# Attention output of a two-block model on one core: split value and probability parts in fp32r, transposes one key block ahead, convolution taps moved

## The chip, the cores and the metric

The kernel runs on one core of one Trainium2 chip. The metric is the time of one execution on the device in microseconds (us). TensorE (PE) does the matrix products and the transposes, VectorE (DVE) and ScalarE (ACT) the elementwise work, SyncE (SP) issues the weight loads.

## The reference, cut to what matters

The model has a first block (gated delta rule heads and pooling, not touched here) and a second block of two layers. Each layer of the second block is a feed-forward part, a mixer, a second feed-forward part and a gated projection, on 512 tokens of width 1024 in float32. The mixer is this:

```python
def forgetting_attention(q, k, v, f_logit):          # 8 heads of 64, 512 tokens
    c = jnp.cumsum(jax.nn.log_sigmoid(f_logit), axis=1)
    for blk in range(s // Q_BLOCK):                  # 4 query blocks of 128
        sc = q_blk @ k[:qe].T * scale + (c_q - c_k)  # causal: keys up to qe
        pr = jax.nn.softmax(where(causal, sc, -inf), axis=-1)
        outs.append(pr @ v[:qe])
...
y_attn = forgetting_attention(q, k, v, f_logit) @ w_attn_out
y_conv = silu(rmsnorm(depthwise_conv31(a * sigmoid(b)))) @ w_conv_out   # 512 channels, 31 taps
merged = sigmoid(z_ga) * y_attn + sigmoid(z_gc) * y_conv
return merged @ w_out
```

## The kernel before

Activations lie transposed, 128 channels on the partitions and 512 tokens along the free axis. A weight product is three fp32r products (`mm3`, lines 156 to 158): each float32 operand is split into a high part, rounded to fp32r, and a low part, the rest, and high by high, low by high and high by low are added in PSUM. The weights stream through `Stream`: SP loads a group, ACT casts the high part (`whi`, line 108), DVE subtracts for the low part (`wlo`, line 109).

In `mixer` the order of the code is: four `glu` steps that make the inputs of the convolution, the value product over all heads (`vps`, lines 500 to 507), the copy of the four value tiles from PSUM (`vt`, line 510, one ACT instruction of 512 columns for each), the forget gate (`pf`, lines 513 to 528), then four pairs of heads (`heads`, hp 0 to 3). After these come 16 gate products and 16 output products (`gate`, `part`), interleaved with a distance of `AHEAD` = 3, then `w_out`.

The convolution is 124 DVE instructions a layer ("taps", lines 414 and 419; four channel blocks of 31). They are put into the code in portions: `TAPS0` = 12 after each `glu`, `TAPSV` = 8 after the value product, `TAPS1` = 1, 1, 2, 1 behind the four score blocks of each pair of heads, `TAPS2` = 12 behind each of the attention's output products, and what is left in `conv_out` (line 562), which then squares, sums, normalises, applies silu and splits the result into `yh` and `yl`. `conv_out` stands ahead of part number `CONV_AT` = 5. The first product that reads `yh` and `yl` is part 8.

A pair of heads has two stages. The score stage runs over four query blocks: for each head a score product in two fp32r instructions (`sc`, lines 452 and 454) and a mask product (458), a maximum (DVE, 460), an exponential with its sum (ACT, 462), a reciprocal (463) and a scaling (467). The output stage runs over four key blocks: float32 transposes of the probabilities into PSUM (`pt`, line 477, ten for each head), a DVE copy into SBUF (481), and a float32 product for each head into 64 rows of one PSUM tile (`o`, line 485), so that the two heads take two column halves of the array. Each of these float32 products stands in the trace as two load and matmul pairs. At the end `split` writes the high and low parts `oh` and `ol` (168, 169).

`FILL` says how many steps of the next pair's query and key products (`qk_steps`, 16 steps; for the last pair 8 steps of the first gate product) the code puts behind each score block and each key block. PSUM has two pools of four banks each: `acc` (`psum`) for the weight products, `aux` (`paux`) for scores, transposes and, before, the attention output. The temporaries (`tmp`, among them the gates) share six slots.

The framework in which the kernel is written decides the final order of each engine's instructions when it is built: it follows the order of the code, and pulls later work forward where its plan has an engine free. So the code gives precedence, not the final order. On the chip each engine then works through its list in that order.

Of the kernel before, what the change touches and what calls it, by code (L numbers as in the profile page):

```python
# [7 lines left out]
F32 = mybir.dt.float32  # L8
F32R = mybir.dt.float32r
AF = mybir.ActivationFunctionType  # L10
ALU = mybir.AluOpType
PSUM = bass.MemoryType.PSUM

P = 128
# [6 lines left out]
GRP = 8  # L21
UNIT = 4
AHEAD = 3
ENG2 = dict(pe="v", dup="a", pt="vv")
BANKS2 = (4, 4)
TAPS0 = 12
TAPSV = 8
GATES0 = 1
FILL = (3, 4, 3, 0, 1, 2, 1, 2)
TAPS1 = (1, 1, 2, 1)  # L30
TAPS2 = 12
CONV_AT = 5
NEG = -float(2 ** 100)
EPS = 1e-6

# [117 lines left out]
def mm3(nc, ps, w, x, start, stop):  # L153
    wh, wl = w
    xh, xl = x
    nc.tensor.matmul(ps, lhsT=wh, rhs=xh, start=start, stop=False)  # L156
    nc.tensor.matmul(ps, lhsT=wh, rhs=xl, start=False, stop=False)  # L157
    nc.tensor.matmul(ps, lhsT=wl, rhs=xh, start=False, stop=stop)  # L158
# [8 lines left out]
def split(nc, hi, lo, src):  # L167
    nc.scalar.copy(hi, src)
    nc.vector.tensor_tensor(lo, src, hi.bitcast(F32), op=ALU.subtract)
# [7 lines left out]
def block2(tc, kk, W, h, xp, x0, sq0, p_t, par, out_t):  # L177


    nc = tc.nc  # L180
    with ExitStack() as ctx:
# [15 lines left out]
        def tmp(name="t", shape=(P, S), dt=F32):  # L197
            return tp.tile(list(shape), dt, tag="t", name=name, bufs=NB)

        def psum(name):  # L200
            return acc.tile([P, S], F32, tag="acc", name=name)

        def paux(name, shape=(P, S)):
            return aux.tile(list(shape), F32, tag="aux", name=name)
# [21 lines left out]
        def mtile(i, name, dt=F32R):  # L226
            return mp.tile([P, S], dt, tag=f"m{i}", name=name)
# [37 lines left out]
        def proj(name, l, col, ps=None, k_n=KD, x=None):  # L265
            ps = psum("pj") if ps is None else ps
            x = (xh, xl) if x is None else x
            for k in range(k_n):
                w = W.get((name, l, k * P, col))
                mm3(nc, ps, w, (x[0][k], x[1][k]), k == 0, k == k_n - 1)  # L270
            return ps
# [86 lines left out]
        def gt(i, hl, name):  # L358
            return gp.tile([P, S], F32R, tag=f"g{hl}{i}", name=name)

        def mixer(l, after):
            R = norm()
            oh = [gt(i, "h", f"oh{i}") for i in range(4)]
            ol = [gt(i, "l", f"ol{i}") for i in range(4)]
# [27 lines left out]
            def dup(dst, src):  # L392
                if ENG2["dup"] == "a":
                    nc.scalar.copy(dst, src)
                elif ENG2["dup"] == "p":
                    nc.gpsimd.tensor_copy(dst, src)
                else:
                    nc.vector.tensor_copy(dst, src)
# [29 lines left out]
            def taps(n):  # L428

                while n > 0 and done[0] < 31 * len(ca):  # L430
                    next(conv)
                    done[0] += 1
                    n -= 1
                if done[0] == 124:
                    next(conv, None)

            def heads(hp, qk1, filler):

                rr = [slice(64 * i, 64 * i + 64) for i in range(2)]

                def fill(n):
                    for _ in range(n):
                        next(filler, None)

                pp = [[], []]
                for qb in range(4):
                    n = (qb + 1) * P
                    qs = slice(qb * P, qb * P + P)
                    pss = [paux("sc") for i in range(2)]
                    for i, ps in enumerate(pss):  # L450
                        q, k = qk1[i]
                        nc.tensor.matmul(ps[:, :n], lhsT=q[:, qs], rhs=k[:, :n], start=True, stop=False)
                        q, k = qk2[hp % 2][i]
                        nc.tensor.matmul(ps[:, :n], lhsT=q[:, qs], rhs=k[:, :n], start=False, stop=False)
                    fill(FILL[qb])
                    for i, ps in enumerate(pss):
                        o = ps[:, :n]
                        nc.tensor.matmul(ps[:, qs], lhsT=kk.identr, rhs=maskr, start=False, stop=True)
                        sm = sp.tile([P, 4], F32, tag="sm", name="sm", bufs=4)
                        nc.vector.tensor_reduce(sm[:, 0:1], o, axis=mybir.AxisListType.X, op=ALU.max, negate=True)  # L460
                        pe = cp.tile([P, n], F32, tag=f"pe{qb}", name="pe", bufs=2)
                        nc.scalar.activation(pe, o, AF.Exp, bias=sm[:, 0:1], accum_out=sm[:, 1:2])
                        nc.vector.reciprocal(sm[:, 2:3], sm[:, 1:2])
                        if ENG2["pe"] == "a":
                            nc.scalar.activation(pe, pe, AF.Copy, scale=sm[:, 2:3])
                        else:
                            nc.vector.tensor_scalar(pe, pe, sm[:, 2:3], None, op0=ALU.mult)
                        pp[i].append(pe)
                    taps(TAPS1[qb])
                po_ = paux("o")  # L470
                for kb in range(4):
                    n = S - kb * P
                    pts = []
                    for i in range(2):
                        ps = paux("pt")
                        for qb in range(kb, 4):
                            nc.tensor.transpose(ps[:, (qb - kb) * P:(qb - kb) * P + P], pp[i][qb][:, kb * P:kb * P + P],
                                                kk.ident)
                        t = mtile(8 + kb % 2 * 4 + 2 * i, "pt", F32)[:, :n]
                        copy = nc.scalar.copy if ENG2["pt"][i] == "a" else nc.vector.tensor_copy  # L480
                        copy(t, ps[:, :n])
                        pts.append(t)
                    fill(FILL[4 + kb])
                    for i, r in enumerate(rr):
                        nc.tensor.matmul(po_[r, kb * P:], lhsT=vt[kb][:, hp * P + 64 * i:hp * P + 64 * i + 64], rhs=pts[i],  # L485
                                         start=kb == 0, stop=kb == 3)
                split(nc, oh[hp], ol[hp], po_)

            for cb in range(4):
                glu(cb)  # L490
# [3 lines left out]
            for t in range(4):  # L494
                nc.tensor.matmul(pst[:, 2 * t:2 * t + 2], lhsT=st.sq[:, t * P:t * P + P],
                                 rhs=kk.ones[1024][:, 0:2], start=True, stop=True)
            Rt = sp.tile([P, 8], F32, tag="Rt", name="Rt")
            rstd(Rt, pst)

            vps = [psum(f"v{t}") for t in range(4)]  # L500
            for k in range(KD):
                wh, wl = W.get(("w_in_2", l, k * P, 1024), 4)
                for t in range(4):
# [1 line left out]
                    nc.tensor.matmul(vps[t], lhsT=xh[k][:, ts], rhs=wh, start=k == 0, stop=False)  # L505
                    nc.tensor.matmul(vps[t], lhsT=xl[k][:, ts], rhs=wh, start=False, stop=False)
                    nc.tensor.matmul(vps[t], lhsT=xh[k][:, ts], rhs=wl, start=False, stop=k == KD - 1)
            vt = [mtile(t, f"vt{t}", F32) for t in range(4)]
            for t in range(4):
                nc.scalar.activation(vt[t], vps[t], AF.Copy, scale=Rt[:, 2 * t:2 * t + 1])  # L510
            taps(TAPSV)

            pf = proj("f_2", l, 0)
            z = tmp("z")[0:72]
            nc.vector.tensor_tensor(z, pf[0:72], R[0:72], op=ALU.mult)
            bf = par[0:72, po["b_f"][0] + l:po["b_f"][0] + l + 1]
# [1 line left out]
            e = tmp("e")[0:72]  # L518
# [5 lines left out]
            c = tmp("c")[0:72]  # L524
# [15 lines left out]
            def gate(i):  # L540
                for _ in gate_steps(i):
                    pass
# [8 lines left out]
            for hp in range(4):  # L551
                nxt = [], []
# [9 lines left out]
            def conv_out():  # L562
                taps(200)
                sq = tmp("ysq")
                nc.scalar.activation(sq, y[0], AF.Square)
                for cb in range(1, 4):
                    t = tmp("ysqm")
                    nc.scalar.activation(t, y[cb], AF.Square)
                    nc.vector.tensor_tensor(sq, sq, t, op=ALU.add)
                Rc = norm(sq, 512)  # L570
                yh = [mtile(8 + t, f"yh{t}") for t in range(4)]
                yl = [mtile(12 + t, f"yl{t}") for t in range(4)]
                for cb in range(4):
                    nc.vector.scalar_tensor_tensor(y[cb], y[cb], pcol("g_conv", l, cb), Rc, op0=ALU.mult, op1=ALU.mult)
                    nc.scalar.activation(y[cb], y[cb], AF.Silu)
                    split(nc, yh[cb], yl[cb], y[cb])
                ysp[:] = yh, yl
# [19 lines left out]
            for i in range(2 * KD + AHEAD):  # L597
                if GATES0 <= i < 2 * KD:
                    gate(i)
                if i == CONV_AT + AHEAD:  # L600
                    conv_out()
                if i >= AHEAD:
                    part(i - AHEAD)
            for m in range(KD):
                ps = proj("w_out_2", l, m * P, x=(mh, ml))
# [37 lines left out]
        v = sp.tile([P, 4], F32, name="lv")  # L643
        r = sp.tile([P, 4], F32, name="lr")
# [3 lines left out]
        for m in range(KD):  # L648
            t = tmp("fin")
# [929 lines left out]
```

## Time and profile before

| | |
|---|---|
| median of 3 runs | 2983.38 us (2982.89 to 2984.37) |
| the profiled execution's own time | 2982.64 us |
| its span, first to last instruction | 2980.9 us |
| mean granted TensorE clock | 0.995 |
| PE, DVE, ACT busy, share of the span | 98%, 64%, 44% |

The heads of layer 1 lie at about 1178 to 1269 us of the span, those of layer 2 at about 2297 to 2388 us. A matmul's busy time overlaps that of the next one; what it costs TensorE is the distance from its start to the start of the next instruction. Starts in a row are in us from the span's start; the "idle before" in brackets is the time that the engine had been idle, and what ended it.

### The profile page before, as it was taken

The numbers are of one execution on the slowest core, as the hardware profiler recorded it, in microseconds if no ns is written. First come the engines' busy times: TensorE is split into PE (matmuls) and PEld (weight loads), VectorE is DVE, ScalarE is ACT, GpSimd is POOL, SyncE is SP. The second block draws the span as 40 slices with busy tenths as digits, with TensorE's granted clock in tenths as the row PEclk, the third lists the DMA queues.
The fourth block names the chain that finished last, engine by engine and source line by source line (L and its number), as shares of the span: only waits on it lengthen the run. The fifth ranks groups of instructions, "written<-read, shape, count | busy, mean of one in ns | idle before, by whom it ended". The sixth has DMA issues, their size and how long they took to land.

```text
span 2980.9 us, 37957 instructions
## 1 busy us (share of the span) xinstructions
PE 2935.6 (98%) x13980; PEld 2393.3 (80%) x13980; DVE 1914.2 (64%) x3778; ACT 1302.4 (44%) x2395; POOL 48.1 (2%) x105
## 2 busy tenths in 40 slices
PE   7999999999999999999999999999999999999998
PEld 4888888778888887688888888888888688888886
DVE  6788888777544469886543447544469886543446
ACT  5667766435323335544432335323335544432333
POOL 1000000000000000000000000000000000000000
PEclk9999999999999999999999999999999999999999
DMA  5211123332333332123333333333332123233232
GB/s 202 67 46 46 45 57 106 93 92 90 94 99 95 97 99 85 50 85 99 93 99 99 95 96 101 98 99 97 95 99 84 50 87 99 92 99 99 93 99 85
DMA packets 112970, 268.77 MB, mean 90 GB/s; under 512 B 43536, under 2 KB 47120, under 8 KB 112784
## 3 DMA queue, kind: packets, MB, share of 16 engines
q1 hardware_dynamic: 111760, 266.28, 28.9%
q8 instruction: 110, 1.80, 0.3%
q14 instruction: 76, 0.62, 0.1%
q0 software_dynamic: 1024, 0.07, 0.0%
HBM read 262.17 MB, written 4.06 MB: 89 GB/s over the span
## 4 chain that ended last, share of the span: by engine, by line
PE 95%; DVE 2%; ACT 2%; issue 1%; DMA 0%; DVEq 0%; SPq 0%; ACTq 0%
PE pj L158 17%; PE pj L156 17%; PE pj L157 17%; PE fo L156 5%; PE fo L158 5%; PE fo L157 5%; PE px L156 3%; PE px L157 3%; PE px L158 3%; PE o L485 1%; PE wo L157 1%; PE mP L1268 1%; PE mX L1263 1%; PE wo L158 1%; PE wo L156 1%; PE chn L1315 1%
## 5 line engine op out<-in xcount | busy, mean ns | idle before, releaser
L108 ACT CAST whi<-wraw 128x512 fp32r<-128x512 f32 x914 | 567.0, 621 | 1158.5 <-PE pj L157 700.3
L109 DVE TENSOR_TENSOR wlo<-wraw,whi 128x512 fp32r<-128x512 f32 x914 | 627.4, 687 | 449.4 <-ACT whi L108 427.0
L157 PE MATMUL pj<-xl,whi 128*128 128x512 f32 x1712 | 673.3, 393 | 0.0
L156 PE MATMUL pj<-xh,whi 128*128 128x512 f32 x1712 | 671.1, 392 | 0.9 <-DVE h L1504 0.9
L158 PE MATMUL pj<-xh,wlo 128*128 128x512 f32 x1712 | 670.2, 391 | 0.0
L158 PEld LDWEIGHTS pj<-xh,wlo 128*128 128x128 f32 x1712 | 322.2, 188 | 67.8 <-issue 2.3
L157 PEld LDWEIGHTS pj<-xl,whi 128*128 128x128 f32 x1712 | 322.3, 188 | 66.8 <-issue 2.7
L156 PEld LDWEIGHTS pj<-xh,whi 128*128 128x128 f32 x1712 | 322.4, 188 | 65.9 <-ACT whi L108 1.3
L157 PE MATMUL fo<-gl,whi 128*128 128x512 f32 x704 | 274.1, 389 | 0.0
L158 PE MATMUL fo<-gh,wlo 128*128 128x512 f32 x704 | 274.1, 389 | 0.0
L156 PE MATMUL fo<-gh,whi 128*128 128x512 f32 x704 | 274.1, 389 | 0.0
L419 DVE SCALAR_TENSOR_TENSOR cy<-ca,par,cy 128x489 f32<-128x489 f32 (+17 forms) x240 | 169.5, 729 | 1.5
L157 PE MATMUL px<-xl,whi 128*128 128x512 f32 x392 | 160.3, 409 | 0.0
L158 PE MATMUL px<-xh,wlo 128*128 128x512 f32 x392 | 160.0, 408 | 0.0
L156 PE MATMUL px<-xh,whi 128*128 128x512 f32 x392 | 159.2, 406 | 0.0
L158 PEld LDWEIGHTS fo<-gh,wlo 128*128 128x128 f32 x704 | 132.2, 188 | 27.4
L157 PEld LDWEIGHTS fo<-gl,whi 128*128 128x128 f32 x704 | 132.2, 188 | 27.4
L156 PEld LDWEIGHTS fo<-gh,whi 128*128 128x128 f32 x704 | 132.2, 188 | 27.3
L340 DVE TENSOR_TENSOR fb<-pj,R 128x512 f32<-128x512 f32 x88 | 60.8, 691 | 129.3 <-PE pj L158 129.3
L337 DVE TENSOR_TENSOR fa<-pj,R 128x512 f32<-128x512 f32 x88 | 60.8, 691 | 125.2 <-PE pj L158 123.2
L156 PE MATMUL pj<-nh,whi 128*128 128x512 f32 x352 | 137.5, 391 | 0.0
L157 PE MATMUL pj<-nl,whi 128*128 128x512 f32 x352 | 137.2, 390 | 0.0
(431 smaller groups left out, 4486.3 us busy)
## 6 DMA issues: line engine op xcount, KB each, us to landing
wraw<-in_w_dram SPq DMA_DIRECT2D x465, 512.0 KB
mw<-in_w_dram SPq DMA_DIRECT2D x16, 512.0 KB
raw<-in_xt_dram SPq DMA_DIRECT2D x8, 256.0 KB
h<-in_xt_dram SPq DMA_DIRECT2D x8, 256.0 KB
out_dram<-fin SPq DMA_DIRECT2D x8, 256.0 KB
rawc<-in_ctxt_dram SPq DMA_DIRECT2D x2, 512.0 KB
db<-B SPq DMA_DIRECT2D x64, 6.0 KB
Pm<-dq SPq DMA_DIRECT2D x64, 12.0 KB
```

The costliest lines, as they stand in the source:

```text
L108: nc.scalar.copy(hi, src)
L109: nc.vector.tensor_tensor(lo, src, hi.bitcast(F32), op=ALU.subtract)
L156: nc.tensor.matmul(ps, lhsT=wh, rhs=xh, start=start, stop=False)
L157: nc.tensor.matmul(ps, lhsT=wh, rhs=xl, start=False, stop=False)
L158: nc.tensor.matmul(ps, lhsT=wl, rhs=xh, start=False, stop=stop)
L337: nc.vector.tensor_tensor(a, pa, R, op=ALU.mult)
L340: nc.vector.tensor_tensor(b, pb, R, op=ALU.mult)
L419: nc.vector.scalar_tensor_tensor(yy[:, s:], ca[cb][:, :S - s], pcol("conv_w", l, cb, j), yy[:, s:], op0=ALU.mult, op1=ALU.add)
L485: nc.tensor.matmul(po_[r, kb * P:], lhsT=vt[kb][:, hp * P + 64 * i:hp * P + 64 * i + 64], rhs=pts[i], start=kb == 0, stop=kb == 3)
L1263: nc.tensor.matmul(pX[:, o], lhsT=st.B[:, m0 + m], rhs=alt(st.Q, m0 + m), start=True, stop=True)
L1268: nc.tensor.matmul(pP[:, o], lhsT=Xt[:, m], rhs=alt(st.P, m0 + m), start=True, stop=True)
L1315: nc.tensor.matmul(pa, lhsT=st.kN[:, c], rhs=y2, start=True, stop=True)
```

## The change

The float32 output products become fp32r products. The values are split once a layer into high and low parts that lie side by side: for head i of a pair, `v2` gives a 128-column weight of the 64 high and the 64 low columns (the high half on the rows of that head). The probabilities are split on their way out of PSUM (`split`: ACT cast, then DVE subtraction) in place of the DVE copy. Each head and key block takes two matmuls, the high and the low part of the probabilities against the 128-column weight, into a PSUM tile of its own per head, from the `acc` pool. At the end of a pair, ACT copies the low half's sum to the head's rows, DVE adds the high half's sum, and `split` follows as before. The transposes of key block kb + 1 are put ahead of the products of key block kb. The taps behind the score blocks are dropped (`TAPS1`), `CONV_AT` goes from 5 to 6, the second half of `FILL` (behind the key blocks) from 1, 2, 1, 2 to 2, 1, 2, 1, and the forget gate's product takes an `aux` bank.

```diff
--- before.py
+++ after.py
@@ -21,15 +21,14 @@
 GRP = 8
 UNIT = 4
 AHEAD = 3
-ENG2 = dict(pe="v", dup="a", pt="vv")
+ENG2 = dict(pe="v", dup="a")
 BANKS2 = (4, 4)
 TAPS0 = 12
 TAPSV = 8
 GATES0 = 1
-FILL = (3, 4, 3, 0, 1, 2, 1, 2)
-TAPS1 = (1, 1, 2, 1)
+FILL = (3, 4, 3, 0, 2, 1, 2, 1)
 TAPS2 = 12
-CONV_AT = 5
+CONV_AT = 6
 NEG = -float(2 ** 100)
 EPS = 1e-6
 
@@ -466,9 +465,10 @@
                         else:
                             nc.vector.tensor_scalar(pe, pe, sm[:, 2:3], None, op0=ALU.mult)
                         pp[i].append(pe)
-                    taps(TAPS1[qb])
-                po_ = paux("o")
-                for kb in range(4):
+                po_ = [psum(f"o{i}") for i in range(2)]
+
+                def turned(kb):
+
                     n = S - kb * P
                     pts = []
                     for i in range(2):
@@ -476,15 +476,25 @@
                         for qb in range(kb, 4):
                             nc.tensor.transpose(ps[:, (qb - kb) * P:(qb - kb) * P + P], pp[i][qb][:, kb * P:kb * P + P],
                                                 kk.ident)
-                        t = mtile(8 + kb % 2 * 4 + 2 * i, "pt", F32)[:, :n]
-                        copy = nc.scalar.copy if ENG2["pt"][i] == "a" else nc.vector.tensor_copy
-                        copy(t, ps[:, :n])
+                        t = [mtile(8 + kb % 2 * 4 + 2 * i + j, "pt")[:, :n] for j in range(2)]
+                        split(nc, t[0], t[1], ps[:, :n])
                         pts.append(t)
+                    return pts
+
+                pts = turned(0)
+                for kb in range(4):
+                    nxt = turned(kb + 1) if kb < 3 else None
                     fill(FILL[4 + kb])
-                    for i, r in enumerate(rr):
-                        nc.tensor.matmul(po_[r, kb * P:], lhsT=vt[kb][:, hp * P + 64 * i:hp * P + 64 * i + 64], rhs=pts[i],
-                                         start=kb == 0, stop=kb == 3)
-                split(nc, oh[hp], ol[hp], po_)
+                    for i in range(2):
+                        for j in range(2):
+                            nc.tensor.matmul(po_[i][:, kb * P:], lhsT=v2(kb, 2 * hp + i), rhs=pts[i][j],
+                                             start=kb == 0 and j == 0, stop=kb == 3 and j == 1)
+                    pts = nxt
+                t = tmp("ov")
+                for i, r in enumerate(rr):
+                    nc.scalar.copy(t[r], po_[i][rr[1 - i]])
+                    nc.vector.tensor_tensor(t[r], t[r], po_[i][r], op=ALU.add)
+                split(nc, oh[hp], ol[hp], t)
 
             for cb in range(4):
                 glu(cb)
@@ -505,12 +515,24 @@
                     nc.tensor.matmul(vps[t], lhsT=xh[k][:, ts], rhs=wh, start=k == 0, stop=False)
                     nc.tensor.matmul(vps[t], lhsT=xl[k][:, ts], rhs=wh, start=False, stop=False)
                     nc.tensor.matmul(vps[t], lhsT=xh[k][:, ts], rhs=wl, start=False, stop=k == KD - 1)
-            vt = [mtile(t, f"vt{t}", F32) for t in range(4)]
+
+
+            vt = [[mtile(2 * t + i, f"vt{t}{i}") for i in range(2)] for t in range(4)]
+
+            def v2(t, hd):
+                return vt[t][hd % 2][:, hd // 2 * P:hd // 2 * P + P]
+
             for t in range(4):
-                nc.scalar.activation(vt[t], vps[t], AF.Copy, scale=Rt[:, 2 * t:2 * t + 1])
+                for i in range(2):
+                    b = vt[t][i].rearrange("p (a s c) -> p a s c", s=2, c=64)
+                    hi, lo = b[:, :, i], b[:, :, 1 - i]
+                    src = vps[t].rearrange("p (a e c) -> p a e c", e=2, c=64)[:, :, i]
+                    sc = Rt[:, 2 * t:2 * t + 1]
+                    nc.scalar.activation(hi, src, AF.Copy, scale=sc)
+                    nc.vector.scalar_tensor_tensor(lo, src, sc, hi.bitcast(F32), op0=ALU.mult, op1=ALU.subtract)
             taps(TAPSV)
 
-            pf = proj("f_2", l, 0)
+            pf = proj("f_2", l, 0, ps=paux("pf"))
             z = tmp("z")[0:72]
             nc.vector.tensor_tensor(z, pf[0:72], R[0:72], op=ALU.mult)
             bf = par[0:72, po["b_f"][0] + l:po["b_f"][0] + l + 1]
```

## Rows read from the trace of the kernel before

**Rows 1.** The page: span, busy time of PE, chain that ended last by engine.

```profile
span 2980.9 us, 37957 instructions
...
PE 2935.6 (98%) x13980; PEld 2393.3 (80%) x13980; DVE 1914.2 (64%) x3778; ACT 1302.4 (44%) x2395; POOL 48.1 (2%) x105
...
PE 95%; DVE 2%; ACT 2%; issue 1%; DMA 0%; DVEq 0%; SPq 0%; ACTq 0%
```

**Rows 2.** Chain that ended last, by line, heads of layer 1 (1178.1 to 1268.8).

```profile
by line: PE o L485 17.5%; PE pj L157 13.6%; PE pj L158 13.3%; PE pt L477 13.1%; PE pj L156 13.0%; PE sc L452 5.8%; PE sc L454 4.4%; ACT qk L381 3.4%; DVE cy L419 2.9%; PE sc L458 2.7%; ACT q L394 2.1%; ACT pe L462 1.5%; DVE qk L376 1.4%; DV
```

**Rows 3.** Windows over the heads of layers 1 and 2, busy time of each engine.

```profile
1178.10:1268.80 90.70, 89.31 (x430) 60.81 (x430) 81.55 (x194) 51.20 (x115) 3.83 (x8) 0.98 0.18 53
2297.50:2388.20 90.70, 89.71 (x427) 61.28 (x427) 80.23 (x192) 50.00 (x114) 3.84 (x8) 0.97 0.16 52
```

**Rows 4.** Timeline of PE: output products of 384 columns, one head, then both.

```profile
1197.13 0.86 PE L485 MATMUL o<-pt,vt 128*64 128x384 f32 x2
1197.92 0.33 PE L477 MATMUL pt<-ident,pe 128*128 128x128 f32 x1
...
1220.60 0.87 PE L485 MATMUL o<-pt,vt 128*64 128x384 f32 x4
1221.39 0.55 PE L477 MATMUL pt<-ident,pe 128*128 128x128 f32 x3
```

**Rows 5.** Timeline of PE: starts of fp32r matmuls of 128, 256, 384, 512 columns.

```profile
1247.06 0.28 PE L458 MATMUL sc<-maskr,identr 128*128 128x128 f32 x1
1247.17 0.28 PE L454 MATMUL sc<-k,q 66*128 66x128 f32 x1
...
1248.39 0.29 PE L452 MATMUL sc<-qk,qk 128*128 128x256 f32 x1
1248.51 0.28 PE L454 MATMUL sc<-k,q 66*128 66x256 f32 x1
...
1249.50 0.34 PE L454 MATMUL sc<-k,q 66*128 66x384 f32 x1
1249.68 0.34 PE L452 MATMUL sc<-qk,qk 128*128 128x384 f32 x1
...
1271.18 0.39 PE L156 MATMUL pj<-xh,whi 128*128 128x512 f32 x1
1271.41 0.39 PE L157 MATMUL pj<-xl,whi 128*128 128x512 f32 x1
```

**Rows 6.** Waits of the weight loads in the heads of layer 1.

```profile
PEld o L485 <- DVE pt L481: 2.4, 8, 0.4
```

**Rows 7.** Groups by form, heads of layer 1: busy us, mean ns, idle before.

```profile
L481 DVE COPY pt<-pt 128x512 f32<-128x512 f32 x8 | 5.3, 684 | 0.3 <-PE pt L477 0.2
...
L394 ACT CAST q<-qk 64x512 fp32r<-64x512 f32 x6 | 3.7, 619 | 0.1
...
L481 DVE COPY pt<-pt 128x256 f32<-128x256 f32 x8 | 3.3, 417 | 0.8 <-PE pt L477 0.7
...
L536 DVE TENSOR_TENSOR ga<-pj,R 128x512 f32<-128x512 f32 x2 | 1.4, 676 | 0.0
```

**Rows 8.** Windows of the taps of line 419 alone, layer 1: DVE busy (count).

```profile
1153.00:1178.00 25.00, 13.05 (x19) 1.00 0.31 85
1178.10:1268.80 90.70, 16.99 (x24) 0.98 0.18 53
1268.80:1310.00 41.20, 23.81 (x34) 1.00 0.29 88
```

**Rows 9.** Timeline behind the heads: last tap, first square, low parts, their first reader.

```profile
1307.30 0.72 DVE L419 SCALAR_TENSOR_TENSOR cy<-ca,par,cy 128x482 f32<-128x482 f32 x1
...
1317.24 0.63 ACT L565 ACTIVATE ysq<-cy 128x512 f32<-128x512 f32 x1
...
1338.41 1.29 DVE L169 TENSOR_TENSOR yl<-cy,yh 128x512 fp32r<-128x512 f32 x2
...
1342.29 0.39 PE L156 MATMUL pj<-yh,whi 128*128 128x512 f32 x1
```

## The prediction

> **What bounds the kernel now.** I read the page first. TensorE is busy for 98% of the span, and 95% of the chain that ended last is TensorE's [rows 1], so time taken off TensorE's list is time saved, unless something else then ends last. The change touches one part of the mixer, twice: the heads of each layer, 90.7 us in both [rows 3], so I read those stretches instead of the page's averages. The same chain, cut to the heads of layer 1, gives the output products 17.5% [rows 2]: 0.175 x 90.7 = 15.9 us. Adding up the TensorE lines that the row names gives some 83%, so about 15 us of this stretch ran over ACT, DVE and issue, and the taps alone hold 2.9% of it, 2.6 us. The windows say how near the others are: DVE 81.6 of 90.7 us, ACT 51.2 [rows 3]. So the heads are a stretch in which TensorE sets the time and DVE is a close second, while the page's 64% for DVE hides it.
>
> Layer 2 repeats layer 1 within 1.3 us in each window [rows 3]; I work out one layer and double it.
>
> **The output products.** A float32 product of 384 columns for one head holds TensorE from 1197.13 to 1197.92, 0.79 us; both heads together, issued side by side, hold it from 1220.60 to 1221.39, again 0.79 us [rows 4]. So the second head is free when it directly follows the first, and costs the full price when it does not. The new products are fp32r with 128 weight columns, two for each head and key block, as many instructions as before: 16 of each width in a layer (4 pairs x 2 heads x 2 parts). Their nearest rows are fp32r products of the same widths: 0.11, 0.12, 0.18 and 0.23 us from start to start [rows 5]. Sum: 16 x 0.64 = 10.2 us. Against the 15.9 us that the old ones hold on the chain this is -5.7 us.
>
> The Trainium skill, TensorEngine Tiling (Array Packing), under Overview (Theoretical Speedup), gives a dimension of at most 64 up to twice the speed, and this change gives up exactly that packing. Where the two heads stand side by side the rows agree with it (0.79 us for one or two); by the rule for all products the old ones would cost about 10.2 x 0.79/0.72 = 11.2 us and the gain would shrink to 1.0 us, against 5.7 us by the chain.
>
> **The waits of the heads.** What the taps held of the chain, 2.6 us, should go when nothing forces a tap between a maximum and a scaling; I take -2.6. The transposes ahead can also remove the 2.4 us in which loads of the output product waited for the copy of `pt` [rows 6]; but part of that lies under matmuls that were still running, so it only widens the bound: 0 (other waits of the softmax take over the taps' place) to -5.0. Late next is then the softmax itself, which must still be finished before the first transpose of a pair.
>
> **The extra elementwise work.** The DVE copy becomes a DVE subtraction of the same shape: 0.68 us at 512 columns, 0.42 at 256 [rows 7]; no subtraction out of PSUM with these widths is in the trace, and I take the copy's price. New on DVE are two additions of 64 rows by 512 for each pair, at most 2 x 0.68, so 1.4 us a pair and 5.5 us a layer. Without taps DVE held 81.6 - 17.0 = 64.6 us [rows 3, 8]; the new sum is 70.1 us. ACT gets 8 casts and 2 copies a pair; at 0.62 us each as an upper bound, the price of a 512-column copy between halves [rows 7], that is 25 us a layer on top of 51.2. Both stay under the 82 us that remain, so I cost them at nothing in the heads; the cover is TensorE's own 74 to 82 us, and without it they would cost their 5.5 us. The cast stands ahead of the subtraction, so a pair's probabilities are ready some 0.6 us later than with one copy; the transposes of the next block and one or two fill steps (three matmuls of 0.23 each) lie in between. Behind a late cast ACT's exponentials and `qk` copies would queue. At the end of a pair the chain of copy, addition and split is longer by about 2 us; its reader comes after the heads, and `acc` has two more banks for the next products, so nothing.
>
> **The value split.** Four ACT copies become eight halves, and DVE gets eight subtractions of 256 columns: 8 x 0.42 = 3.3 us. In the 25 us ahead of the heads DVE ran 19 taps [rows 8], which can step back: five of them, at 0.7 us (23.81/34), pay for it. I take 0, with 3.3 us as the end if the first scores have to wait for it. The forget gate's other bank moves nothing that waits.
>
> **Where the taps go.** This is the cost. In layer 1, 24 taps ran in the heads and 34 behind them, the last ending at 1308.0, 39.2 us after the heads: 0.87 taps per us with DVE full [rows 8, 9]. In the new heads DVE has 82 - 70 = 12 us free, but it also stood idle for 9 us before, with taps at hand; I allow 7 taps. Behind the heads then remain 34 + 24 - 7 + 5 = 56 taps, 64.6 us. The first reader of `yl` started 73.5 us after the heads (1342.29 - 1268.8), and from the first square to the first low part it took from 1317.24 to about 1339.1, 21.9 us [rows 9]. 64.6 + 21.9 = 86.5 us: 13.0 us late. Against that, one gate product (24 matmuls x 0.23 = 5.4 us) can be run ahead of part 8: of the two gates finished in the heads of layer 1 [rows 7] the code asks for one there, so such pulling happens. And DVE is no longer full once the taps are over, so the chain of 21.9 us can tighten, and the squares of the first three channel blocks needn't wait for the last tap. Ends: 0 and 7.6 us; I take +3, below the middle for these two reasons.
>
> **Sum.** -5.7 - 2.6 + 0 + 3 = -5.3 us a layer, -10.6 us in all. The profiled execution took 2982.64 us (span 2980.9 and 1.7 around it), 0.7 below the median of the runs. 2982.64 - 10.6 = 2972.0 us.
>
> **The rivals.**
> - More is gained: the convolution is hidden wholly and the waits for `pt` go too: -10.7 us a layer, 2961 us. For it: DVE idles a good part of the time after 1308; against it: the 13 us above. Chance 0.14.
> - The heads do not get shorter: what the products free turns into waits for softmax and the two-step split, since ACT and DVE each get more to do in strict order. Then the convolution isn't late either, because part 8 stays where it was: 2982.6 us. For it: the 15 us of the chain on other engines [rows 2]; against it: both engines have room. Chance 0.12.
> - The old products were nearly free as pairs, so that only 1.0 us goes: -0.6 us a layer, 2981.4 us. Against it stands their 15.9 us on the chain. Chance 0.05.
> - Slower: the convolution ends last. Place: part 8, which waits for `yh` and `yl`. If the heads take no tap at all, 63 remain, 72.6 us, and with the old 21.9 us the first low part comes at 94.5, 21.0 late, 15.6 after a gate is pulled: +7.3 us a layer, 2997 us. It decides from the point where the lateness left passes 8.3 us, what the heads gain, which is at 57 taps if nothing in the chain tightens. My own estimate is 56. Chance 0.13.
> - The forecast has 0.56.
>
> **Numbers.** Bounds: -5.7 - 5.0 + 0 = -10.7 and -5.7 + 0 + 7.6 = +1.9 us a layer, 2961 to 2986; that leaves out the slow rival and little else, so 2961 to 2986 is the range. 0.2% is 6 us, about what the measurement can tell from no change. Faster by more: the forecast and the first rival, 0.70; within: 0.17; slower: 0.13.
>
> **What would show it.** Right: line 485's successor holds some 10 us of the chain in a layer's heads, the heads take 81 to 83 us, fp32r products of 128 weight columns start 0.11 to 0.23 us apart, the tap line is gone from that chain. The convolution: a wait of TensorE's weight load ahead of the first product on `yh`, 1 to 5 us, or a gate product run ahead of it. Wrong: heads of 88 us or more with TensorE waiting for `pe`, `pt` or the new low part; or taps that run on past 60 us behind the heads with a TensorE gap of 8 us or more; or TensorE's granted clock at its lower level (1.2 GHz) after such a gap, which would put the time above the range.

## The result, and the profile after

The changed kernel takes 3013.49 us (median of 4 runs, 3012.05 to 3015.71) against 2983.25 before (4 runs): ratio 1.0103, 95% interval 1.0091 to 1.0115. It is 30 us slower, where 10.6 us less was forecast. The profiled execution took 3012.05 us.

The page after, span and busy time, beside [rows 1]:

```profile
span 3010.4 us, 38040 instructions
...
PE 2943.3 (98%) x13980; PEld 2411.4 (80%) x13980; DVE 1931.1 (64%) x3810; ACT 1339.1 (44%) x2483; POOL 48.0 (2%) x105
```

TensorE runs the same 13980 matmuls and is 98% busy again; the page says nothing of where 29.5 us of span went. The windows over the heads do: layer 1 at the place of [rows 3], layer 2 where its heads now lie (columns: busy us and count for PE, PEld, DVE, ACT, POOL, then clock, DMA share, GB/s):

```profile
1178.10:1268.80 90.70, 80.78 (x388) 61.17 (x389) 85.08 (x199) 63.72 (x149) 4.60 (x10) 0.92 0.14 42
2310.00:2401.30 91.30, 81.92 (x387) 62.73 (x388) 85.05 (x199) 63.49 (x148) 4.59 (x10) 0.91 0.13 41
```

The heads are as long as before (first score at 1178.1, last output product at 1268.5), TensorE is busy 8.5 us less in them, and 388 matmuls run there instead of 430. The window of layer 1 for the weight products alone (tile `pj`), before:

```profile
1178.10:1268.80 90.70, 53.84 (x190) 33.25 (x190) 5.44 (x8) 0.98 0.18 53
```

and after:

```profile
1178.10:1268.80 90.70, 42.26 (x148) 26.76 (x149) 4.74 (x7) 0.92 0.14 42
```

All 42 missing matmuls are weight products, 9.7 us of work at 0.23 us each [rows 5]. They had filled TensorE while a pair's softmax was still running; now they come behind the heads. Most of them are missing in the last pair. Weight products from 1253.0 to 1268.0, before, then after (the two counted there are the ends of products that started earlier):

```profile
1253.00:1268.00 15.00, 10.19 (x38) 6.47 (x38) 0.67 (x1) 1.00 0.25 70
...
1253.00:1268.00 15.00, 0.37 (x2) 0.00 (x0) 0.67 (x1) 0.66 0.00 0
```

The first product on `oh` starts at 1285.1 instead of 1275.9, 9.2 us later. What TensorE waits for instead, in the heads of layer 1 after:

```profile
PE pt L477 <- ACT pe L461: 4.5, 3, 3.1
PE sc L451 <- ACT qk L393: 2.2, 5, 1.1
PE o L490 <- ACT pt L167: 2.0, 4, 0.6
...
PE o L490 <- DVE pt L168: 0.3, 2, 0.2
```

The longest wait stands in the last pair. Timelines of PE, then ACT, after:

```profile
1255.21 0.23 PE L457 MATMUL sc<-maskr,identr 128*128 128x128 f32 x1
1258.56 3.50 PE L477 MATMUL pt<-ident,pe 128*128 128x128 f32 x12 [3.13 <-ACT pe L461]
1262.53 0.80 PE L490 MATMUL o<-pt,vt 128*128 128x512 f32 x1 [0.46 <-ACT pt L167]
```

```profile
1254.60 1.28 ACT L559 ACT_TABLE_LOAD   x1
1255.89 0.63 ACT L559 ACTIVATE ga<-ga 128x512 f32<-128x512 f32 x1
1256.54 1.28 ACT L461 ACT_TABLE_LOAD   x1
1257.84 0.58 ACT L461 ACTIVATE pe<-sc,sm 128x384 f32<-128x384 f32 x1
```

A gate's sigmoid with its two table loads (3.2 us) sits between the exponentials. It sat there before too (1252.26 to 1255.50), but TensorE then had products of the gates to run through it. In the wait of 3.13 us the granted clock falls to its lower level (1.2 GHz), and it stays there after it:

```profile
1247.00:1257.00 10.00, 7.86 (x39) 6.10 (x39) 9.91 (x25) 7.20 (x16) 0.00 (x0) 1.00 0.18 55
1257.00:1269.00 12.00, 9.93 (x38) 7.07 (x39) 9.62 (x23) 7.07 (x18) 0.00 (x0) 0.57 0.00 0
```

A mean of 0.57 over 12 us means 0.43 x 12 = 5.2 us of full clock missing, so some 10.3 us at half speed. Behind the heads stand the rows that answer [rows 8] and [rows 9]: tap windows (line 418 now), which show the heads and the stretch behind them, then the last tap, the first square and the first reader of `yh`:

```profile
1178.10:1268.80 90.70, 18.49 (x26) 0.92 0.14 42
1268.80:1310.00 41.20, 25.69 (x37) 1.00 0.30 89
```

```profile
1308.29 0.71 DVE L418 SCALAR_TENSOR_TENSOR cy<-ca,par,cy 128x482 f32<-128x482 f32 x1
...
1334.54 0.63 ACT L587 ACTIVATE ysq<-cy 128x512 f32<-128x512 f32 x1
...
1355.01 0.50 PE L155 MATMUL pj<-yh,whi 128*128 128x512 f32 x1 [3.50 <-ACT yh L167]
```

The taps did not move: 26 in the heads against 24, and the last one 1.0 us later than before. Yet the first square comes 17.3 us later (1317.24 before), and the first product on `yh`, 12.7 us later than in [rows 9], waits 3.50 us for `yh`, whose making starts with this square. Again the clock falls, this time behind the wait:

```profile
1355.00:1358.00 3.00, 2.77 (x8) 1.80 (x9) 2.21 (x5) 2.98 (x6) 0.00 (x0) 0.72 0.00 0
1358.00:1361.00 3.00, 3.00 (x11) 2.40 (x11) 1.20 (x3) 2.12 (x3) 0.00 (x0) 0.71 0.00 0
1361.00:1364.00 3.00, 3.00 (x15) 2.50 (x14) 2.31 (x4) 1.20 (x2) 0.00 (x0) 1.00 0.45 126
```

At the first product on `mh` layer 1 is 15.0 us late (1400.8 against 1385.8); twice that is the loss.

### The profile page after: what moved, and what is told of

It is laid out like the page before. It is cut to its first block, busy times and chain, and to the rows that moved or that the text cites. A ratio compares the mean times of both kernels' runs of the same rounds, so it can differ in the third digit from the quotient of the medians.

```text
span 3010.4 us, 38040 instructions
## 1 busy us (share of the span) xinstructions
PE 2943.3 (98%) x13980; PEld 2411.4 (80%) x13980; DVE 1931.1 (64%) x3810; ACT 1339.1 (44%) x2483; POOL 48.0 (2%) x105
## 5 line engine op out<-in xcount | busy, mean ns | idle before, releaser
L156 PE MATMUL pj<-xl,whi 128*128 128x512 f32 x1696 | 665.1, 392 | 0.0
L155 PE MATMUL pj<-xh,whi 128*128 128x512 f32 x1696 | 664.0, 392 | 0.9 <-DVE h L1526 0.9
L157 PE MATMUL pj<-xh,wlo 128*128 128x512 f32 x1696 | 662.5, 391 | 0.0
L418 DVE SCALAR_TENSOR_TENSOR cy<-ca,par,cy 128x507 f32<-128x507 f32 (+18 forms) x240 | 170.1, 729 | 1.2
```

The lines of the kernel that those rows point to most:

```text
L418: nc.vector.scalar_tensor_tensor(yy[:, s:], ca[cb][:, :S - s], pcol("conv_w", l, cb, j), yy[:, s:], op0=ALU.mult, op1=ALU.add)
```

## The experiments

The first theory (A) was that the output tiles, now from the pool of the weight products, keep those products out of the heads; the second (B), that the convolution ends late, from the taps (B2) or from the place of `conv_out` (B1). The rival to A was that the split of the probabilities, or the transposes ahead, make the softmax chain longer. Differences from the kernel before are taken against its runs beside the same experiment (medians 2983.3 to 2983.6 us).

**Output tiles in banks of their own** (from the changed kernel; the value product takes two of these banks, so that the total of eight stays):

```diff
-BANKS2 = (4, 4)
+BANKS2 = (3, 3)
+opool = ctx.enter_context(tc.tile_pool(name="b2o", bufs=1, space=PSUM))
-po_ = [psum(f"o{i}") for i in range(2)]
+po_ = [opool.tile([P, S], F32, tag=f"o{i}", name=f"o{i}") for i in range(2)]
-vps = [psum(f"v{t}") for t in range(4)]
+vps = [psum(f"v{t}") for t in range(2)] + [opool.tile([P, S], F32, tag=f"o{t}", name=f"v{2 + t}") for t in range(2)]
```

> The changed kernel, with the two output tiles of a pair in two PSUM banks of their own; the weight products (acc) and the scores and transposes (aux) have three banks each in place of four. The output is the same. Theory A (the output tiles in the acc pool keep the gate products from being pulled into the heads, so TensorE has nothing to run while the softmax works, worst in the last pair): the order of the changed kernel holds 147 weight-product matmuls between the first score and the last output product of a layer, before it was 189, here it is 182; 35 x 0.23 = 8 us a layer should come back, and the 3.1 us wait ahead of the last pair's transposes with the half clock behind it should go: 2990 to 2997 us. Theory B (the taps that moved make the convolution late): the heads' part changes nothing of that, and the time stays at 3008 to 3014, or the convolution takes back what the heads give. Theory C (the two-step split and the transposes ahead make the softmax chain longer): 3010 to 3016, and worse with one bank less for scores and transposes.

Measured 2990.33 us, 1.0023 (1.0013 to 1.0032): 23.2 us less than the changed kernel. Weight products in the heads of layer 1, which here end at 1264.5, 4.0 us earlier than in the changed kernel; the second window closes with them:

```profile
1178.10:1268.80 90.70, 58.96 (x201) 35.87 (x200) 5.96 (x9) 0.96 0.17 52
...
1177.50:1264.70 87.20, 55.28 (x183) 32.78 (x184) 4.76 (x7) 0.96 0.16 49
```

Within the heads that is 35 more than after, 8.1 us at 0.23. With the 4.0 us this makes the 12.1 us by which the first product on `oh` starts earlier (1273.0). A holds.

**The taps and `conv_out` back** (from the changed kernel):

```diff
-CONV_AT = 6
+CONV_AT = 5
                         pp[i].append(pe)
+                    taps((1, 1, 2, 1)[qb])
```

> The changed kernel with the taps behind the score blocks again (1, 1, 2, 1) and the convolution's end ahead of part 5. The output is the same. Theory B: the 3.7 us wait ahead of the first product on yh and the half clock behind it (together about 6 us a layer) go: about 3001 us. Theory A: the heads keep their 147 weight-product matmuls, so 9 us a layer stay lost whatever the taps do; 3001 at best, 3010 or more if DVE's taps delay the softmax again as they did before.

Measured 3000.59 us, 1.0059 (1.0044 to 1.0074): 12.9 us less than the changed kernel.

**Taps and `conv_out` moved alone** (from the kernel before):

```diff
-TAPS1 = (1, 1, 2, 1)
+TAPS1 = (0, 0, 0, 0)
-CONV_AT = 5
+CONV_AT = 6
```

> The kernel before, with only the taps moved: none behind the score blocks, the convolution's end ahead of part 6. The output is the same. Theory B: slower than before by what the convolution lost in the changed kernel, 6 us a layer: about 2995 us. Theory A: the heads keep their 189 weight-product matmuls, DVE has none of the extra additions and subtractions, so the convolution is late by less: 2980 to 2990 us.

Measured 2996.05 us, 1.0043 (1.0026 to 1.0060): the same 12.7 us without any new product, so B is independent of A.

**No transposes ahead** (from the changed kernel):

```diff
-pts = turned(0)
 for kb in range(4):
-    nxt = turned(kb + 1) if kb < 3 else None
+    pts = turned(kb)
...
-    pts = nxt
```

> The changed kernel without the transposes one key block ahead: each block's transposes and split stand just before its products. The output is the same. Theory C: if the transposes ahead are what makes the chain longer, this is faster than the changed kernel by several us (3005 or less). Theory A and B: it is the same within 4 us or slower (3011 to 3020), since each product then waits for its own split of two steps, 0.6 us longer than the copy.

Measured 3013.31 us in a single run, inside the spread of the changed kernel's four: no cost or gain of the transposes ahead shows there.

**`CONV_AT` = 6 alone** (from the kernel before; the one line of the diff above)

> The kernel before, with the convolution's end ahead of part 6 in place of part 5; the taps stay behind the score blocks. The output is the same. Theory B1 (the place of the convolution's end in the code alone makes it late: in the run with both edits the last tap ended as early as before, near 1309 us, but the first square started 10 us later): 2996 us, as with both edits. Theory B2 (the taps dropped behind the score blocks are what makes it late): 2983 us.

Measured 2995.46 us, 1.0041 (1.0026 to 1.0056). **`TAPS1` to zero alone** (from the kernel before; the other line)

> The kernel before, without the taps behind the score blocks; the convolution's end stays ahead of part 5. The output is the same. Theory B1: 2983 us, since the taps are pulled into the heads as before (25 of them). Theory B2: 2996 us. If the taps did cost the heads their 2.6 us on the chain and now step back: 2978 us.

Measured 2983.29 us, 1.0000 (0.9990 to 1.0010). So it is B1 and not B2. The timelines of `CONV_AT` = 6 alone:

```profile
1309.42 0.72 DVE L419 SCALAR_TENSOR_TENSOR cy<-ca,par,cy 128x482 f32<-128x482 f32 x1
...
1327.00 0.62 ACT L108 CAST whi<-wraw 128x512 fp32r<-128x512 f32 x1 [2.04 <-PE pj L157]
1327.53 0.63 ACT L565 ACTIVATE ysq<-cy 128x512 f32<-128x512 f32 x1
...
1348.07 0.79 PE L156 MATMUL pj<-yh,whi 128*128 128x512 f32 x1 [3.50 <-ACT yh L168]
```

The last tap is 2.1 us later than before [rows 9], the first square 10.3 us: what was waited for was not the taps but the turn of the square in ACT's list. The square starts with no idle time of ACT right behind a weight cast, and that cast had waited 2.04 us for a weight product on TensorE. The line of the code puts one gate and one part more ahead of the square (36 matmuls of 0.23, 8.3 us); the taps' 2.1 us and these 8.3 us come to about the 10.3. The window around the end of the 3.50 us wait shows the clock:

```profile
1347.00:1357.00 10.00, 8.93 (x25) 6.82 (x26) 6.06 (x10) 7.00 (x12) 0.00 (x0) 0.66 0.06 11
```

**Both repaired**: own banks and `CONV_AT` = 5, on the changed kernel

> The changed kernel with the output tiles in two PSUM banks of their own (three for acc, three for aux) and the convolution's end ahead of part 5 again. The output is the same. Theories A and B1 together: the 23 us that the banks gave back and the 13 us of the convolution add up, 3013 - 36 = 2977 us, so faster than the kernel before by 6 us: what the fp32r products save once nothing else is lost. If the convolution's end can't be hidden at its old place either, since DVE has more to do: 2983 to 2990.

Measured 2977.22 us, 0.9980 (0.9971 to 0.9989), faster than both kernels. The two repairs add up: 3013.49 - 23.2 - 12.9 = 2977.4. The heads of layer 1 take 86.2 us (1178.0 to 1264.2). The chain over the window of [rows 2], which here reaches 4.6 us past them:

```profile
by line: PE pj L157 13.9%; PE pj L156 13.7%; PE pj L155 13.2%; PE o L491 12.0%; PE pt L478 10.0%; PE sc L452 6.7%; PE sc L454 4.3%; ACT qk L381 3.4%; ACT qk L394 3.3%; ACT ov L496 3.2%; DVE wlo L108 2.3%; ACT whi L107 2.1%; ACT pe L462 2.1%
```

and its square and first product on `yh`, with no wait ahead of it:

```profile
1314.05 0.63 ACT L588 ACTIVATE ysq<-cy 128x512 f32<-128x512 f32 x1
...
1339.08 0.39 PE L155 MATMUL pj<-yh,whi 128*128 128x512 f32 x1
```

**The float32 products in own banks** (from the kernel before, with the `BANKS2`, `opool` and `vps` lines of the first experiment, and this one):

```diff
-po_ = paux("o")
+po_ = opool.tile([P, S], F32, tag=f"o{hp % 2}", name="o")
```

> The kernel before with its float32 output products, but with the output tile in two PSUM banks of its own and three banks each for acc and aux. The output is the same. If the bank split by itself gives something: 2978 or less, and the fp32r products are worth nothing beside it. If three banks in place of four cost something: 2985 to 2990, and the fp32r products saved more than the 6 us. Theory A says nothing of it but that no weight product is kept out of the heads: 204 of them are planned there, 189 before.

Measured 2989.80 us, 1.0020 (1.0011 to 1.0030), on the same chip as the 2977.22. Splitting the banks 3, 3 and 2 costs 6.5 us by itself; on equal banks the new products, the split and the transposes ahead gain 12.6 us. The dropped `TAPS1`, the moved `FILL` and the forget gate's bank are in this difference too; of these only `TAPS1` was run by itself, with no effect.

**More gate products by the code** (changed kernel, `GATES0` from 1 to 3, so that the last pair's fill does not run dry)

> The changed kernel, banks untouched, but with three gate products in place of one handed to the last pair as its fill by the code. The output is the same. This separates two readings of theory A: 171 weight-product matmuls are now planned between the first score and the last output product of a layer, against 147 (before: 189), with the output tiles still in the acc pool. If the missing weight products are the cause: 24 x 0.23 = 5.5 us a layer, and the 3.1 us wait of the last pair with its half clock gone: 2996 to 3003 us. If the shared banks cost in another way (products waiting for a bank): 3010 or more.

Measured 3000.27 us, 1.0054 (1.0039 to 1.0069), 13.2 us less than the changed kernel. Weight products in the heads of layer 1:

```profile
1178.10:1268.80 90.70, 48.80 (x171) 30.83 (x171) 4.74 (x7) 0.94 0.15 47
```

The output tiles are still in `acc` here, so more filling by itself brings back part of the loss.

**The repaired kernel without the transposes ahead** (edit as above)

> The kernel of the run with own banks and the convolution's end ahead of part 5, without the transposes one key block ahead. The output is the same. If the transposes ahead are worth the 2 us a layer of waits on the copy: 2981 us. If more weight products fit in between when they are not ahead (198 are planned in the heads, 182 with them ahead): 2977 or less.

Measured 2979.07 us, 0.9987 (0.9978 to 0.9996). The 1.9 us lie within the two intervals, and the runs come from two chips: the transposes ahead are worth little, about that or nothing.

**The repaired kernel with `CONV_AT` = 4**

> The kernel of the run with own banks and the convolution's end ahead of part 5, now ahead of part 4. The output is the same. If something of the convolution is still late there: faster than 2977. If it is hidden at part 5: the same. The taps that are still open by then would be forced into the line ahead of the gates: up to 5 us slower.

Measured 2978.24 us, 0.9982 (0.9973 to 0.9991): once the square's turn is not late, an earlier turn brings nothing.

**The repaired kernel with banks 4, 2 and 2** (`BANKS2 = (4, 2)`, `vps` as in the changed kernel)

> The kernel of the run with own banks and the convolution's end ahead of part 5, with four banks for acc and two for the scores and transposes. The output is the same. 228 weight-product matmuls are planned in the heads, 182 with three and three. If the fourth acc bank is worth more than the third bank of the scores: 2970 or less; the score waits with two banks (a score block needs both at once) speak against it: 2985 or more.

Measured 2996.58 us, 1.0043 (1.0028 to 1.0057). Its heads end late, by the lines of tile `o` (start of the first and the last):

```profile
L491 PE MATMUL o<-pt,vt x64: 221/385/792, 1195.7 to 1286.2; 128*128 128x512 f32 x16, 128*128 128x384 f32 x16, 128*128 128x256 f32 x16, 128*128 128x128 f32 x16
```

With 220 weight products between 1178.1 and 1268.8, more fill went ahead of the last pair's output products, the last of which came 17.7 us after its place in the changed kernel. So more fill is not better without end. Whether the fourth `acc` bank or the missing third `aux` bank stretched the heads was not separated.

**The pool alone** (from the kernel before, the float32 products and all else kept):

```diff
-po_ = paux("o")
+po_ = psum("o")
```

> The kernel before with one line changed: the float32 output tile of a pair is taken from the acc pool in place of the aux pool. Products, transposes, taps and the convolution's place are as before, and the output is the same. Theory A in its pure form (a tile of the acc pool that stands ahead of the gates in the code keeps them from being pulled forward): 152 weight-product matmuls are planned in the heads in place of 189, 37 x 0.23 = 8.5 us a layer, 3000 us, up to 3008 with a wait and half clock in the last pair. If the fp32r products or the two-step split had part in the changed kernel's loss of the heads: 2983 to 2993.

Measured 3005.43 us, 1.0073 (1.0056 to 1.0090): 22 us lost by one word. Heads of layer 1, all tiles over the usual window, then `pj` alone from the first score to the last output product of this run (1179.3 to 1272.1):

```profile
1178.10:1268.80 90.70, 79.40 (x379) 53.14 (x379) 83.15 (x195) 47.74 (x112) 3.83 (x8) 0.96 0.13 42
...
1179.20:1272.30 93.10, 42.78 (x152) 26.73 (x152) 4.79 (x7) 0.96 0.13 40
```

and its longest wait there:

```profile
PE pt L477 <- ACT pe L462: 4.6, 5, 3.4
```

That is 38 weight products fewer than before, nearly the loss of the changed kernel (42), and a wait for the softmax like its own (3.4 us at most, 3.1 there), with none of the split, the fp32r products or the transposes ahead. The rival to A falls: the pool does it. In this run the taps hold 10.8% of the chain over the usual window, against 2.9% before [rows 2]; what share DVE has in the waits here was not separated.

## Why the prediction was wrong, step by step

**The step that failed on the larger part** is one that was passed over inside "The extra elementwise work": of the output tiles' new pool it says only "`acc` has two more banks for the next products, so nothing". The pool was counted in banks at the end of a pair. What it decides is which later work the build may pull forward: with the output tiles in `acc`, a layer's heads got 148 weight products instead of 190. With the float32 products kept, that word alone costs 22 us (3005.43); in the changed kernel it costs 23.2 against tiles in banks of their own (2990.33), a step that changes the bank split too. That it is the pool is shown. The weight products in the heads were planned as 147 (changed kernel), 182 (own banks) and 152 (the pool alone), and the traces show 148, 183 and 152, so the order is made when the kernel is built and not by waits on the chip. Why the build comes to this order is argued: the gate products take their tiles from the same pool and stand behind the output tiles in the code. The prediction worked out that TensorE sets the time in the heads, but not that 190 of its 430 matmuls there were weight products, of the next pair and of the gates, which fill the waits and so make it so.

**"Where the taps go"** failed for the other part. It forecast 56 taps behind the heads and +3 us a layer; 37 ran there, the last tap ended 40.2 us after the heads instead of 64.6, and dropping `TAPS1` changed nothing (1.0000), since the order pulled the taps into the heads anyway. What cost time was `CONV_AT`, which the step did not price: 12.1 us by that line alone, of the 12.7 us with both. The rival "Slower: the convolution ends last" had the place right, part 8, where TensorE waited 3.50 us for `yh`, but not the cause: it decides by the number of taps, and the taps were on time.

**"The output products"** were nearly right. In the repaired kernel they hold 12.0% of the chain over the same window, 0.120 x 90.7 = 10.9 us; 10.2 was worked out, against 15.9 before [rows 2]. The kernel before also differs in the banks, so the time is compared with the float32 products in own banks: 12.6 us gained, where -5.7 and -2.6 a layer, 16.6 in all, were forecast for these products and **"The waits of the heads"**. The direction holds, the sum was 4 us too large; the heads, forecast at 81 to 83 us, take 86.2. On that chain the taps' 2.9% are gone, as forecast, but ACT's copy of the low half's sum (`ov`) has 3.2%, which was put outside. The -2.6 us for the taps does not come from dropping `TAPS1`: with that line alone the taps keep their 2.9% of the chain, and the time stays. The rival that the old products were nearly free as pairs, -1.2 us in all, is refused by the same 12.6 us. The Trainium skill, TensorEngine Tiling (Array Packing), under Overview (Theoretical Speedup), gives such packing up to twice the speed. By that rule the prediction worked out a gain of 1.0 us a layer; the two chains here show 15.9 - 10.9 = 5.0 us.

**"The extra elementwise work"** and **"The value split"**, by price, from the groups by form after:

```profile
L168 DVE TENSOR_TENSOR pt<-pt 128x512 fp32r<-128x512 f32 x8 | 5.4, 686 | 0.7 <-ACT pt L167 0.5
...
L168 DVE TENSOR_TENSOR pt<-pt 128x256 fp32r<-128x256 f32 x8 | 3.4, 425 | 1.7 <-PE o L490 0.7 <-ACT pt L167 0.7
L532 DVE SCALAR_TENSOR_TENSOR vt<-v,Rt,vt 128x256 fp32r<-128x256 f32 x8 | 3.4, 478 | 0.0
```

The subtraction out of PSUM costs what the copy did (686 and 425 ns, 0.68 and 0.42 taken [rows 7]), the value split 3.4 us on DVE where 3.3 stood. The first scores did not wait for it (1178.1 in both kernels). The prediction says that the trace before holds no such subtraction, but it holds one at 512 columns, `ol<-o,oh` (line 169), at 691 ns.

**"The heads do not get shorter"** described the heads that came (90.4 us, waits for `pe` and `pt`), but for another reason and with the wrong time: it kept the total at 2982.6, since it did not see that the heads were losing the weight products that fill them. Of the signs listed as showing the prediction wrong, one came as written: heads of 88 us or more with waits for `pe` and `pt`. The clock at 1.2 GHz came too, but with gaps of 3.1 and 3.5 us, where one of 8 us or more was named.

From the kernel before to the changed one the runs make a path of single steps: own banks for the output tiles +6.5 (2983.3 to 2989.8), new products with the split, the transposes ahead and the rest of the change -12.6 (to 2977.22), `CONV_AT` +13.1 (to 2990.33), output tiles into `acc` and the banks back to four and four +23.2 (to 3013.49).

## What to carry to other kernels

Where later work fills the waits of a stretch, ask of every edit what it does to that filling before counting instructions: count the matmuls in the stretch that belong to something else, and see which pool their tiles come from and what stands ahead of them there. A place in the code is priced by the turn that the step's first instruction gets in its engine's list, not by when its inputs are ready; here the last tap was done 25 us before the first square ran. Change the pool and the mathematics apart: the new products, with what came beside them, were worth 12.6 us, and one word for a pool hid it.

## What the runs showed of the hardware

Around an idle stretch of TensorE of 3.13 us the granted clock was at its lower level for some 10.3 us (0.43 missing of 12 us, at half speed), in a stretch of short matmuls with further waits. Around a wait of 3.50 us ahead of `yh` it was there for some 3.4 us (0.28 and 0.29 missing of 3 us each) in the changed kernel and for 6.8 us (0.34 of 10 us) with `CONV_AT` = 6 alone. So the same wait of 3.50 us went with different lengths, and a wait's price is not its own length. The transposes, the same instructions in both kernels, hold 10.0% of the chain in the repaired kernel and 13.1% before [rows 2]; whether this comes from the products around them was not measured.
